# Down-projections over all inner tiles in one span, with four PSUM banks open for each product

## The chip, the core and the metric

The kernel runs on one core of a Trainium2 chip. TensorE (PE in the profile) multiplies into PSUM, VectorE (DVE), ScalarE (ACT) and GpSimd (POOL) work on tiles in SBUF and PSUM, SyncE (SP) issues the loads and stores. The metric is the device time of one execution in microseconds; below, the median of three runs and one profiled execution.

## The reference

Two transformer blocks in a row on 1024 tokens of 1024 features, all in float32. The first has a sliding-window attention beside a gated convolution, the second three kinds of attention and a cross attention. Each ends in a gated feed-forward part with 2816 inner features, whose last product is what the change is about:

```python
# first block
hn = rms_norm(h, ffn_pre_g)
ff = (jax.nn.silu(hn @ w_gate) * (hn @ w_up)) @ w_down
h = h + rms_norm(ff, ffn_post_g)
...
# second block
h = _rmsnorm(x, norm_ffn[l])
gate, up = jnp.split(h @ w_gu[l], 2, axis=-1)
x = x + (jax.nn.silu(gate) * up) @ w_down[l]
...
return _rmsnorm(x, final_norm)
```

## The kernel before

Activations lie with features on the 128 partitions and 512 tokens (one half) in a tile. For precision every operand of a product is split: `hi` is a cast on ACT (L162, L422), `lo` a subtraction of two SBUF operands on DVE or POOL (L163 for weights, L423 for activations), and `mm3` (L530 on) makes each product of three matmuls: hi by hi, hi by lo, lo by hi (L533, L534, L535).

`lower` (L1376) is the down-projection; it is called at L1603 ("down1", into new tiles `ffacc`) and at L2091 ("down2", added to the residual `res`). Its input, 22 inner tiles of two halves, comes from DRAM (`z`), its weights from a stream in DRAM, in pieces of 4 inner tiles by 128 columns (`W.quarter`, called weight quarters below). It takes Winograd's form of Strassen's algorithm: rows are the two halves of the tokens, the inner dimension has two halves, columns come in pairs, four pairs `q`; seven products replace eight. Their operands are sums of x tiles (tiles `s1` and `ff` on DVE, L1398) and differences of weight quarters (`wt`, `wraw`, DVE, L174).

The 22 inner tiles are taken in three chunks, `CHUNKS`, of 8, 8 and 6: in each, `seven` runs all seven products, here named by their evictions: w1 (`ev1`), w5, w6, w7, w4, and the two last with the plain quarters, w3 and w2. Every product makes for each `q` one PSUM bank of 4 (or 3) inner tiles, 12 (or 9) matmuls in a row, and evicts it: a copy to `u` or to the result on ACT (L1455, L1450), or an addition on DVE (L1398); the sums `c += u` of `ev6` and `ev7` are on POOL (`plus`, L1401), in the last chunk on DVE. A chunk loads each operand once: 92 loads for all three. Which engine splits is set by two lists: weights of `q` in `BYDVE` on DVE, x tiles of number `k` in `XDVE` on DVE, the rest on POOL.

What sets the order: the code emits a stage's operands one stage ahead of its matmuls (`AHEAD` = 1), evictions are emitted with a raised priority (`EVP`), and a scheduler orders each engine's queue by that; every engine then takes its queue in order. Loads all go through SP's one queue. Pools bound how far operands run ahead: 8 raw weight quarters (`wq`), 8 each of split ones (`whi`, `wlo`), 7 PSUM banks (`mm`).

When the last chunk's w4 is done, the half of the tokens that is complete goes on: `then(1)` (`to_second` with the post-norm and the residual, reloaded from DRAM by `reload`, or `finish` with the last norm) is emitted before w3's matmuls; `then(0)` follows the end. In the second call the last product's last chunk runs in two pieces of 256 columns (`TAIL`), so that the last norm starts on the first piece.

Of the kernel before, what the change touches and what calls it, by code (L numbers as in the profile page):

```python
# [17 lines left out]
P = 128  # L18
# [8 lines left out]
CHUNKS = ((0, 4), (8, 4), (16, 3))  # L27
AHEAD = 1
PIPE = "fcm"
BYDVE = (3,)  # L30
XDVE = (1, 3)
# [9 lines left out]
BUFS = {'v': 39, 'u': 8, 'p': 4, 'g': 4, 'mm': 7, 's': 3, 't': 3, 'o': 2, 'tmp': 3, 'evt': 3, 'stg': 2, 'rbc': 3, 'turn': 2, 'pt': 2, 'small': 20, 'csmall': 8, 'wraw': 3, 'whi': 8, 'wlo': 8, 'x': 58, 'y': 16, 'ge': 9, 'wt': 6, 'wq': 8, 'r': 16, 'sum': 4, 'rsum': 3, 'f': 6, 'l': 3}  # L41
NPRE = (4, 2)
TAIL = 2
# [37 lines left out]
# float32 values of 10000 ** (-arange(0, 32, 2) / 32)  # L81
# [16 lines left out]
class Weights:  # L98
    """Weights arrive as one stream of 128x128 blocks in the order of their use."""

    def __init__(self, tc, pool, stream):
        self.tc = tc
        self.nc = tc.nc
        self.last = None
        self.marks = {}
        self.pool = pool
        self.stream = stream
        self.order = []
        self.cur = None
        self.made = 0  # L110
# [4 lines left out]
    def in_turn(self, start):  # L115
        """Loads in the order of the stream."""
# [30 lines left out]
    def quarter(self, mat, k, c0, n=4):  # L147
        """n feature tiles of one column of blocks, as they come."""
        while len(self.order) % 4:
            self.order.append(None)  # L150
        s = len(self.order) // 4
        raw = self.pool.tile([P, 512], F32, tag="wq", name=f"wraw{s}", bufs=BUFS["wq"])[:, :n * P]
        self.load(raw, s, n * P)
        self.order += [(mat, k + i, c0) for i in range(n)] + [None] * (4 - n)
        return raw

    def parted(self, raw, eng=None):
        self.made += 1
        w = raw.shape[-1]
        hi = self.pool.tile([P, 512], F32R, tag="whi", name=f"xhi{self.made}", bufs=BUFS["whi"])[:, :w]  # L160
        lo = self.pool.tile([P, 512], F32R, tag="wlo", name=f"xlo{self.made}", bufs=BUFS["wlo"])[:, :w]
# [16 lines left out]
class Act:  # L178
    """Feature tiles of an operand, split: tile k, token half h -> 512 columns hi, 512 lo."""
# [17 lines left out]
class Rows:  # L197
    """Feature tiles in float32: tile i, token half h -> 512 columns."""
# [14 lines left out]
def weave(main, jobs, per=1.0, start=0):  # L213
    """Emits main's steps with jobs between them: per jobs for each step after the first ones."""
# [39 lines left out]
def merged(main, side, n):  # L254
    """main's steps, with a step of side after every n of them."""
# [7 lines left out]
def piped(makers, depth=1):  # L263
    """Jobs from makers of generators: each starts one and takes the ones before a step on."""
# [19 lines left out]
def encoder_decoder_kernel(ctx: ExitStack, tc: tile.TileContext, a: dict, order_out: list):  # L284
# [25 lines left out]
    def act(name, place="vv"):  # L310
        """place: the kind of slot, a letter for each half, or a function of tile and half."""
# [26 lines left out]
    # constants and columns: slices of two tiles (one of matrix operands); the columns go round  # L338
# [71 lines left out]
    flip = [0]  # L410

    def copy(dst, src):
        """PSUM to SBUF, on the two engines in turn."""
# [6 lines left out]
    def split(hi, lo, src, eng=None):  # L420
        """src = hi + lo exactly, both in 12 significant bits."""
# [3 lines left out]
    class Squares:  # L425
        """Sum of squares of [128, w] tiles; side: in two accumulators until the last one."""
# [32 lines left out]
    class Running:  # L459
        """Sums of squares taken as the rows leave PSUM, for each half."""  # L460
# [23 lines left out]
    def rstd(acc, dim, r=None, psum=sps, late=None):  # L484
        """(column sums of acc / dim + eps) ** -0.5: r [128 tokens, tiles], and on every
# [1747 lines left out]
```

## Time and profile before

| | |
|---|---|
| median of 3 runs | 2506.37 us (2502.11 to 2509.57) |
| profiled execution, span | 2505.9 us |
| PE busy | 2372.9 us, 95% |
| DVE busy | 1894.8 us, 76% |
| POOL busy | 1641.7 us, 66% |
| ACT busy | 1015.9 us, 41% |
| first down-projection | from 908 to 1155 us |
| second down-projection | from 2241 to 2492 us |

The shares are means over many stages. A matmul of 512 columns takes 0.23 us when PE runs dense at the full clock; a longer spacing is a wait or a lower granted clock. For one stage, the table of stretches is to be read: busy time of each engine in it, the clock, and what the loads moved.

### The profile page before, as it was taken

To read this page: it belongs to the slowest core of one execution; us is meant where nothing else is said; L and a number is where in the kernel's file an instruction comes from. 1 tells how busy PE (TensorE), PEld (TensorE's weight loads), DVE (VectorE), ACT (ScalarE), POOL (GpSimd) and SP (SyncE) were. 2 spreads that over 40 slices of the span, in tenths; PEclk is the share of its full clock that TensorE was granted. 3 is DMA by queue.
4 is the path that set the end of the run, shared out by engine and by line. 5 is a ranking of instruction groups with operands and counts; after the bars stand their busy time and mean duration, and the time that the engine had idled before them with its cause. 6 is when DMAs were issued, how large, how long until landed. Compare 5 with 4: busy or idle time off the path is not lost.

```text
span 2505.9 us, 34363 instructions
## 1 busy us (share of the span) xinstructions
PE 2372.9 (95%) x11892; PEld 1908.6 (76%) x11892; DVE 1894.8 (76%) x2784; ACT 1015.9 (41%) x2088; POOL 1641.7 (66%) x1194
## 2 busy tenths in 40 slices
PE   8788999889999999998999999999999999998987
PEld 7666777668888877776878778888878888876766
DVE  7989768999555589999443465676799555579988
ACT  5344754533232243435444353544533222334433
POOL 4657557998766669877522334164489666668885
PEclk9888999999999999999999999999999999999998
DMA  4211126423232233232653448113213222253221
GB/s 144 76 34 34 39 81 213 148 72 118 86 104 80 88 123 105 86 121 95 205 154 113 146 121 280 39 51 95 89 59 105 80 76 88 85 190 103 77 73 67
DMA packets 141421, 259.62 MB, mean 104 GB/s; under 512 B 15712, under 2 KB 28352, under 8 KB 141248
## 3 DMA queue, kind: packets, MB, share of 16 engines
q1 hardware_dynamic: 134512, 235.34, 28.9%
q0 software_dynamic: 6448, 21.91, 2.8%
q8 instruction: 94, 1.54, 0.3%
q14 instruction: 79, 0.65, 0.1%
q10 hardware_dynamic: 288, 0.18, 0.0%
HBM read 188.42 MB, written 68.94 MB: 103 GB/s over the span
## 4 chain that ended last, share of the span: by engine, by line
PE 59%; DVE 14%; issue 3%; POOL 2%; ACT 1%; DMA 1%; SPq 0%; DVEq 0%; POOLq 0%; ACTq 0%
PE p L535 10%; PE p L533 10%; PE p L534 10%; PE mm L533 4%; PE mm L534 4%; PE mm L535 4%; DVE s L1398 2%; PE tp L584 2%; PE low L535 2%; PE low L534 2%; PE low L533 2%; DVE ff L423 2%; DVE wt L174 1%; PE lo L1885 1%; DVE ffacc L1398 1%
## 5 line engine op out<-in xcount | busy, mean ns | idle before, releaser
L163 POOL TENSOR_TENSOR xlo<-wt,xhi 128x512 fp32r<-128x512 f32 (+1 forms) x230 | 358.1, 1575 | 31.7 <-ACT xhi L162 24.0
L163 POOL TENSOR_TENSOR xlo<-wraw,xhi 128x512 fp32r<-128x512 f32 (+1 forms) x204 | 321.3, 1588 | 26.5 <-ACT xhi L162 24.1
L140 POOL TENSOR_TENSOR wlo<-wraw,whi 128x512 fp32r<-128x512 f32 x144 | 205.7, 1437 | 142.1 <-ACT whi L139 120.5
L533 PE MATMUL p<-s,xhi 128*128 128x512 f32 x704 | 278.3, 396 | 1.3 <-DVE u L1292 1.0
L535 PE MATMUL p<-s,xlo 128*128 128x512 f32 x704 | 277.7, 396 | 0.9 <-POOL xlo L163 0.9
L534 PE MATMUL p<-s,xhi 128*128 128x512 f32 x704 | 278.0, 395 | 0.0
L535 PE MATMUL low<-ff,xlo 128*128 128x512 f32 (+1 forms) x628 | 252.9, 403 | 25.2 <-POOL xlo L163 25.2
L534 PE MATMUL low<-ff,xhi 128*128 128x512 f32 (+1 forms) x628 | 251.2, 400 | 6.6 <-DVE ff L423 4.5
L533 PE MATMUL low<-ff,xhi 128*128 128x512 f32 (+1 forms) x628 | 250.5, 400 | 5.5 <-DVE u L1398 3.7
L1301 POOL TENSOR_TENSOR g<-g,rbc 128x512 f32<-128x512 f32 x82 | 116.4, 1421 | 188.2 <-ACT g L1300 188.2
L1300 ACT ACTIVATE g<-g 128x512 f32<-128x512 f32 x82 | 51.9, 633 | 422.2 <-DVE g L1299 413.6
L533 PE MATMUL p<-x,xhi 128*128 128x512 f32 x528 | 210.2, 398 | 5.6 <-ACT early L1300 4.9
L535 PE MATMUL p<-x,xlo 128*128 128x512 f32 x528 | 210.6, 399 | 1.1 <-POOL xlo L163 1.1
L534 PE MATMUL p<-x,xhi 128*128 128x512 f32 x528 | 210.0, 398 | 0.1
L162 ACT CAST xhi<-wt 128x512 fp32r<-128x512 f32 (+1 forms) x248 | 142.6, 606 | 144.0 <-DVE wt L174 103.7
L535 PEld LDWEIGHTS low<-ff,xlo 128*128 128x128 f32 x628 | 122.1, 194 | 59.3 <-POOL xlo L163 32.7
L533 PEld LDWEIGHTS p<-s,xhi 128*128 128x128 f32 x704 | 132.8, 189 | 33.4 <-ACT xhi L162 1.4
L535 PEld LDWEIGHTS p<-s,xlo 128*128 128x128 f32 x704 | 132.6, 188 | 32.6 <-POOL xlo L163 1.8
L534 PEld LDWEIGHTS p<-s,xhi 128*128 128x128 f32 x704 | 132.9, 189 | 31.2
L534 PEld LDWEIGHTS low<-ff,xhi 128*128 128x128 f32 x628 | 122.3, 195 | 35.9 <-DVE ff L423 5.8
L533 PEld LDWEIGHTS low<-ff,xhi 128*128 128x128 f32 x628 | 122.1, 194 | 34.3 <-issue 4.2
L162 ACT CAST xhi<-wraw 128x512 fp32r<-128x512 f32 (+1 forms) x228 | 129.6, 599 | 36.4 <-POOL xlo L163 13.5
(446 smaller groups left out, 6445.9 us busy)
## 6 DMA issues: line engine op xcount, KB each, us to landing
wraw<-wstream SPq DMA_DIRECT2D x408, 256.0 KB, 3.0
ff<-zff SPq DMA_DIRECT2D x88, 256.0 KB, 3.5
zff<-up SPq DMA_DIRECT2D x76, 256.0 KB, 2.0
res<-zres SPq DMA_DIRECT2D x48, 256.0 KB, 5.4
x<-xT SPq DMA_DIRECT2D x32, 256.0 KB, 5.4
zres<-res SPq DMA_DIRECT2D x32, 256.0 KB, 2.0
lqk<-zl POOLq DMA_DIRECT2D x16, 512.0 KB, 6.3
wraw<-wstream SPq DMA_DIRECT2D x32, 192.0 KB, 3.1
```

The costliest lines, as they stand in the source:

```text
L140: self.last_part = nc.gpsimd.tensor_tensor(lo, raw, hi.bitcast(F32), op=ALU.subtract)
L162: self.nc.scalar.copy(hi, raw)
L163: ins = (eng or self.nc.gpsimd).tensor_tensor(lo, raw, hi.bitcast(F32), op=ALU.subtract)
L174: self.nc.vector.tensor_tensor(t, a, b, op=ALU.subtract)
L423: return (eng or nc.gpsimd).tensor_tensor(lo, src, f32(hi), op=ALU.subtract)
L533: nc.tensor.matmul(ps, lhsT=ah, rhs=bh, start=first and i == 0, stop=False)
L534: nc.tensor.matmul(ps, lhsT=ah, rhs=bl, start=False, stop=False)
L535: nc.tensor.matmul(ps, lhsT=al, rhs=bh, start=False, stop=last and i == n - 1)
L584: nc.tensor.transpose(ps[:, tsl(j)], pr[:, c0 + (g + j) * P:][:, :P], ident)
L1300: nc.scalar.activation(t, t, AF.Silu)
L1301: nc.gpsimd.tensor_tensor(t, t, rb_[h], op=ALU.mult)
L1398: nc.vector.tensor_tensor(out, x_, y_, op=op)
```

## The change

The chunks go. `lower` runs the seven products once, each over all 11 tiles of its inner half, in three groups of operands of 4, 4 and 3 tiles. The four column pairs' banks are open together through a product (132 matmuls), and are evicted once, at its end: 48 evictions in a down-projection, not 144. Operands are no longer kept: each product loads what it needs when it needs it, 96 weight quarters and 99 x tiles for each down-projection (before 48 and 44). Only the running differences of the weights (new pool `wk`, 12 quarters) and the sums `s_` are kept and updated in place. `plus` is gone: all `c += u` are on DVE, but for four copies in the first call. `BYDVE` and `XDVE` grow: DVE splits two of four weight quarters and three of four x tiles (`k % 4`). `then(1)` is queued before w3 as before; the residual is reloaded in two parts, in w4 and in w3. In the second call the last product is kept whole (46 tiles of split operands) and runs in two pieces of 256 columns. Comments are cut, which moves line numbers: the split of activations is L428, of weights L168, differences L179, the sums and evictions on DVE L1406.

```diff
-CHUNKS = ((0, 4), (8, 4), (16, 3))
-BYDVE = (3,)
-XDVE = (1, 3)
+BYDVE = (1, 3)
+XDVE = (1, 2, 3)
...
-            ins = split(hi, lo, t, nc.vector if k in XDVE else nc.gpsimd)
+            ins = split(hi, lo, t, nc.vector if k % 4 in XDVE else nc.gpsimd)
...
-        def plus(out, x_, y_, op=ALU.add):
-            nc.gpsimd.tensor_tensor(out, x_, y_, op=op)
...
-                def products():
                     for q in Q4:
-                        hi, lo = wparts[q]
-                        ps = mmps("low")
-                        mm3(ps, [((hi[:, tsl(k)], lo[:, tsl(k)]), parts[k]) for k in K])
-                        with tc.high_priority(offset=EVP):
-                            evac(q, ps)
...
+        def w1(g, q):
+            t[g, q] = block(0, 0, g, q, "wk")
+            return t[g, q]
+
+        def w5(g, q):
+            return W.difference(block(0, 1, g, q), t[g, q], t[g, q])
+
+        def w6(g, q):
+            return W.difference(block(1, 1, g, q), t[g, q], t[g, q])
+
+        def w7(g, q):
+            b22 = block(1, 1, g, q)
+            return W.difference(b22, block(0, 1, g, q), b22)
...
+        def x5(k):
+            s_[k] = load(k, 1)
+            return vec(s_[k], s_[k], load(n + k, 1))
...
+        def ev7(q, ps):
+            vec(u[q], u[q], ps)
+            vec(c(q, 3), c(q, 3), u[q])
+            if fresh:
+                nc.gpsimd.tensor_copy(c(q, 2), u[q])
+            else:
+                vec(c(q, 2), c(q, 2), u[q])
...
+        def operands(w_, x_, g, keep):
+            xs = [parted(x_(k), k) for k in groups[g]]
+            ws = []
+            for q in Q4:
+                into = (xt("wk", F32R), xt("wk", F32R)) if keep else None
+                ws.append(W.parted(w_(g, q), nc.vector if q in BYDVE else None, into))
+            return ws, xs
...
+        def whole(parts, g, ps, ev, done):
+            for q in Q4:
+                if g == 0:
+                    ps[q] = mmps("low")
+                group(ps[q], q, g, parts)
+                if g == G[-1]:
+                    with tc.high_priority(offset=EVP):
+                        ev(q, ps[q])
...
+        for w_, x_, ev, done in products:
+            ps, kept = {}, []
+            if done == 1:
+                soon(lambda: then(1))
+            for g in G:
+                keep = tail and done == 0
+                parts = operands(w_, x_, g, keep)
...
+                if keep:
+                    kept.append(parts)
                 else:
+                    soon(lambda parts=parts, g=g, ps=ps, ev=ev, done=done:
+                         whole(parts, g, ps, ev, done))
```

PE before, inside a product of the first down-projection: the last two inner tiles of one bank, then the next bank from its first tile on (`low_8513` and `low_8527` are banks, `ff` the x parts, `xhi` and `xlo` the weight parts).

```order
L533 MATMUL low_8513<-ff_8357,xhi_8373 128x512
L534 MATMUL low_8513<-ff_8358,xhi_8373 128x512
L535 MATMUL low_8513<-ff_8357,xlo_8374 128x512
L533 MATMUL low_8513<-ff_8361,xhi_8373 128x512
L534 MATMUL low_8513<-ff_8362,xhi_8373 128x512
L535 MATMUL low_8513<-ff_8361,xlo_8374 128x512
L533 MATMUL low_8527<-ff_8349,xhi_8377 128x512
L534 MATMUL low_8527<-ff_8350,xhi_8377 128x512
L535 MATMUL low_8527<-ff_8349,xlo_8378 128x512
```

PE after, at the switch from w6 to w7 in the first down-projection: the last matmuls of w6's banks `low_8662` to `low_8701`, and the first of w7's `low_8999` to `low_9038`.

```order
L539 MATMUL low_8662<-ff_8732,xhi_8738 128x512
L540 MATMUL low_8662<-ff_8731,xlo_8739 128x512
L539 MATMUL low_8675<-ff_8732,xhi_8745 128x512
L540 MATMUL low_8675<-ff_8731,xlo_8746 128x512
L539 MATMUL low_8688<-ff_8732,xhi_8752 128x512
L540 MATMUL low_8688<-ff_8731,xlo_8753 128x512
L539 MATMUL low_8701<-ff_8732,xhi_8759 128x512
L540 MATMUL low_8701<-ff_8731,xlo_8760 128x512
L538 MATMUL low_8999<-ff_8816,xhi_8852 128x512
L538 MATMUL low_9012<-ff_8816,xhi_8861 128x512
L538 MATMUL low_9025<-ff_8816,xhi_8870 128x512
L538 MATMUL low_9038<-ff_8816,xhi_8879 128x512
```

The four banks now take each inner tile in turns and close within eight matmuls; before, one bank closed every twelve.

DVE after, at the same switch: w6's evictions (`u` less a bank, then `ffacc` plus `u`) and what stands between and behind them; `ff_8811` is w7's first x tile, `xlo` are weight splits, `wraw` weight differences.

```order
L428 TENSOR_TENSOR ff_8732<-ff_8413,ff_8731 128x512
L1406 TENSOR_TENSOR u_7925<-u_7925,low_8662 128x512
L1406 TENSOR_TENSOR u_7926<-u_7926,low_8675 128x512
L1406 TENSOR_TENSOR ffacc_8565<-ffacc_8565,u_7925 128x512
L1406 TENSOR_TENSOR u_7927<-u_7927,low_8688 128x512
L1406 TENSOR_TENSOR ff_8811<-ff_8811,ff_8813 128x512
L168 TENSOR_TENSOR xlo_8978<-wraw_8972,xhi_8977 128x512
L1406 TENSOR_TENSOR u_7928<-u_7928,low_8701 128x512
L1406 TENSOR_TENSOR ffacc_8578<-ffacc_8578,u_7926 128x512
L179 TENSOR_TENSOR wraw_9186<-wraw_7953,wraw_9186 128x512
```

The first x tile of the new product is made behind three evictions and an addition. ACT after, at the switch before, from w5 to w6 (`ffacc` copies are w5's evictions, `ff_8501` is the first x cast of w6):

```order
L1456 COPY ffacc_8563<-low_8343 128x512
L1456 COPY ffacc_8565<-low_8343 128x512
L167 CAST xhi_8644<-wraw_8007 128x512
L1456 COPY ffacc_8576<-low_8356 128x512
L1456 COPY ffacc_8578<-low_8356 128x512
L167 CAST xhi_8651<-wraw_8013 128x512
L1456 COPY ffacc_8589<-low_8369 128x512
L1456 COPY ffacc_8591<-low_8369 128x512
L427 CAST ff_8501<-ff_8167 128x512
```

The x cast stands behind six copies and two weight casts. POOL in the middle of the first down-projection, before and then after:

```order
L163 TENSOR_TENSOR xlo_9118<-wt_8747,xhi_9117 128x512
L1401 TENSOR_TENSOR ffacc_8176<-ffacc_8176,u_8629 128x512
L423 TENSOR_TENSOR ff_9294<-ff_9081,ff_9293 128x512
L1401 TENSOR_TENSOR ffacc_8193<-ffacc_8193,u_8630 128x512
L163 TENSOR_TENSOR xlo_9122<-wt_8749,xhi_9121 128x512
```

```order
L428 TENSOR_TENSOR ff_8933<-ff_8927,ff_8932 128x512
L168 TENSOR_TENSOR xlo_9190<-wraw_9186,xhi_9189 128x512
L168 TENSOR_TENSOR xlo_9204<-wraw_9200,xhi_9203 128x512
L428 TENSOR_TENSOR ff_9057<-ff_9051,ff_9056 128x512
L168 TENSOR_TENSOR xlo_9305<-wraw_9301,xhi_9304 128x512
```

The additions to `ffacc` are gone from it, and fewer splits are left.

## Rows read from the trace of the kernel before

**Rows 1.** The page's head and its busy times by engine.
```profile
span 2505.9 us, 34363 instructions
PE 2372.9 (95%) x11892; PEld 1908.6 (76%) x11892; DVE 1894.8 (76%) x2784; ACT 1015.9 (41%) x2088; POOL 1641.7 (66%) x1194
```

**Rows 2.** Stretches: length, busy PE, PEld, DVE, ACT, POOL, clock, DMA share, GB/s.
```profile
700.00:880.00 180.00, 180.00 (x784) 146.05 (x783) 102.45 (x135) 53.56 (x99) 118.96 (x83) 1.00 0.26 88
908.00:1156.00 248.00, 226.44 (x946) 179.17 (x944) 234.82 (x252) 105.25 (x198) 205.91 (x135) 0.97 0.30 96
1156.00:1240.00 84.00, 77.22 (x467) 65.10 (x468) 60.29 (x65) 39.06 (x64) 61.56 (x47) 1.00 0.60 196
...
2240.00:2492.00 252.00, 229.10 (x1000) 182.37 (x998) 240.27 (x269) 99.78 (x189) 203.35 (x129) 0.96 0.26 85
...
2230.00:2240.00 10.00, 10.00 (x45) 8.07 (x44) 8.80 (x9) 4.53 (x8) 8.07 (x6) 1.00 1.04 379
```

**Rows 3.** Splits of L423 from 908 to 1156: min/median/max ns, first and last start.
```profile
L423 POOL TENSOR_TENSOR ff<-ff,ff x22: 1288/1746/1842, 936.2 to 1118.3; 128x512 fp32r<-128x512 f32 x22
...
L423 DVE TENSOR_TENSOR ff<-ff,ff x18: 675/1776/1801, 936.7 to 1117.4; 128x512 fp32r<-128x512 f32 x18
```

**Rows 4.** The tile `low`, whole span, and what ended its engines' idle time.
```profile
L533 PE MATMUL low<-ff,xhi x628: 274/394/632, 908.2 to 2491.1; 128*128 128x512 f32 x151, 128*128 128x256 f32 x6
...
L1398 DVE TENSOR_TENSOR u<-u,low x48: 672/674/690, 944.8 to 2468.4; 128x512 f32<-128x512 f32 x48
...
L1398 DVE TENSOR_TENSOR ffacc<-ffacc,low x36: 672/675/689, 972.1 to 1155.5; 128x512 f32<-128x512 f32 x36
...
L1450 ACT COPY ffacc<-low x12: 589/614/652, 918.3 to 939.1; 128x512 f32<-128x512 f32 x12
...
  POOL xlo L163: 57.8, 31
```

**Rows 5.** Groups by line, DVE and POOL, 908 to 1156: busy us, mean ns, idle before.
```profile
L1398 DVE TENSOR_TENSOR ff<-ff,ff 128x512 f32<-128x512 f32 x11 | 13.8, 1258 | 0.1
...
L1398 DVE TENSOR_TENSOR ffacc<-ffacc,u 128x512 f32<-128x512 f32 x12 | 8.6, 759 | 0.0
...
L1401 POOL TENSOR_TENSOR ffacc<-ffacc,u 128x512 f32<-128x512 f32 x20 | 33.7, 1691 | 2.4 <-DVE u L1398 2.4
```

**Rows 6.** Chain that ended last: start us, us, what; three rows from the middle.
```profile
994.68 1.70 DVE s L1398
996.90 1.19 DVE xlo L163
998.09 1.70 DVE ff L1398
```

**Rows 7.** Waits of PE, then of SP, 908 to 1156: us, times, longest.
```profile
PE low L535 <- POOL xlo L163: 13.0, 7, 4.7
PE bc L494 <- DVE sum L448: 4.4, 1, 4.4
...
SPq L113 <- POOL xlo L163: 47.6, 5, 16.6
```

**Rows 8.** Stretches inside the first down-projection, columns as in rows 2.
```profile
1137.00:1143.00 6.00, 1.57 (x15) 1.03 (x13) 5.90 (x9) 3.31 (x6) 2.42 (x3) 0.96 0.31 107
1143.00:1149.00 6.00, 6.00 (x25) 4.83 (x24) 3.78 (x6) 3.44 (x7) 5.09 (x5) 0.50 0.00 0
...
1000.00:1100.00 100.00, 93.00 (x385) 74.05 (x384) 92.96 (x105) 40.35 (x77) 85.56 (x55) 0.97 0.31 93
```

**Rows 9.** The page's DMA issues: count, KB each, us from issue to landing.
```profile
wraw<-wstream SPq DMA_DIRECT2D x408, 256.0 KB, 3.0
ff<-zff SPq DMA_DIRECT2D x88, 256.0 KB, 3.5
```

More of the change, by code (lines that the diff above doesn't have):

```diff
@@ L108, in __init__ @@
         self.order = []
+        self.slots = {}
         self.cur = None
@@ L1163, in park, with unpark @@
         return z
-    def unpark(z):
-        res = rows("res")
-        for h in (0, 1):
+    def unpark(z, halves=(0, 1), res=None):
+        res = res or rows("res")
+        for h in halves:
             for i in range(8):
@@ L1374, in gated, with lower @@
         return z, mark
-    def lower(z, mark, down, acc, run_, fresh, then, ahead=None, before_last=None):
+    def lower(z, mark, down, acc, run_, fresh, then, ahead=None, again=None):
         late = [None, None]
+        n = NFF // 2
+        groups = [range(g, min(g + 4, n)) for g in range(0, n, 4)]
+        G, Q4 = range(len(groups)), range(4)
         def xt(name, dt=F32):
@@ L1530, in lower, with c, block @@
-        queued = []
-        for n0, n in CHUNKS:
-            for products in seven(n0, n, fresh and n0 == 0, n0 + 2 * n == NFF):
-                queued.append(products)
-                if len(queued) > AHEAD:
-                    queued.pop(0)()
-        for products in queued:
-            products()
+            return out
+        def c(q, j):
+            return acc(2 * q + j % 2, j // 2)
+        def block(row, col, g, q, tag="wq"):
+            ks = groups[g]
+            return W.quarter(down, n * row + ks[0], (2 * q + col) * P, len(ks), tag)
@@ new lines, in operands, with group @@
+        def operands(w_, x_, g, keep):
[5 more added lines that the diff above has]
+            return ws, xs
+        def group(ps, q, g, parts, cols=slice(0, HALF)):
+            ws, xs = parts
+            hi, lo = ws[q]
+            mm3(ps, [((hi[:, tsl(i)], lo[:, tsl(i)]), (xs[i][0][:, cols], xs[i][1][:, cols]))
+                     for i in range(len(xs))], first=g == 0, last=g == G[-1])
@@ new lines, in whole, with pieces @@
+        def whole(parts, g, ps, ev, done):
[6 more added lines that the diff above has]
+                        ev(q, ps[q])
+                        if done is not None:
+                            run_.add(done // 2, c(q, done), nc.vector if done > 1 else None)
+        def pieces(parts):
+            w, ends = HALF // tail, []
+            for p_ in range(tail):
+                cols = slice(p_ * w, p_ * w + w)
+                ps = {}
+                for g in G:
+                    for q in Q4:
+                        if g == 0:
+                            ps[q] = mmps("low")[:, :w]
+                        group(ps[q], q, g, parts[g], cols)
+                        if g == G[-1]:
+                            with tc.high_priority(offset=EVP):
+                                d = c(q, 0)[:, cols]
+                                vec(d, d, ps[q])
+                                run_.piece(0, d, cols, q == 3)
+                ends.append(then(0, cols))
+            for e in ends:
+                e()
@@ L1538, in lower @@
+        if ahead:
+            ahead()
+        for f in queued:
+            f()
+        if tail:
+            pieces(kept)
+        else:
+            then(0)
         return late[1]
@@ L1592, in encoder_decoder_kernel, with reload @@
     hm = act("hm")
-    def reload():
-        nx["x"] = unpark(zres)
+    def reload(part):
+        nx["x"] = unpark(zres, (1 - part,), nx.get("x"))
     def to_second(h):
```

177 lines of the change are left out of this document (66 added, 111 removed).

## Prediction

> **What bounds the kernel now.** I read the table of stretches first, then the rows of the splitting line, the rows of the tile that the change concerns, and last the chain and the waits. Sums are made against the profiled span, 2505.9 us [rows 1]; the median of the three runs is 2506.4, so what lies around the span is under a microsecond, and I carry differences over as they are.
>
> PE is busy for 95% of the span [rows 1], which says nothing on the two down-projections. In a gate stage PE runs dense: 784 matmuls in 180.0 us [rows 2], 0.2296 us each at clock 1.00. A down-projection needs 924 of them (7 products x 4 column pairs x 11 inner tiles x 3 terms): 212.2 us. The second, with some of its matmuls as pieces of 256 columns for the tail, needs as much. But the first `low` matmul starts at 908.2 and the first down-projection's last eviction at 1155.5 [rows 4]: 247 us, 35 more than dense; the second fills the stretch from 2240 to 2492 [rows 2], 251 us of it from its first to its last matmul, 38.5 more. What can be won is there: 73.5 us, and some of the 6.8 us in which PE idles from 1156 to 1240 [rows 2].
>
> What takes the place of PE? From 908 to 1156 DVE is busy 234.8 of 248 us and POOL 205.9 [rows 2], and both run slower than they can: a DVE subtraction of two SBUF operands takes 675 ns at best and 1776 in the median, a POOL one 1288 and 1746 [rows 3], whereas DVE operations with one PSUM operand never leave 672 to 690 ns [rows 4]. So the pair competes for reading SBUF, and a POOL operation costs the pair 1.776 - 0.675 = 1.10 us beside the DVE's 0.675. Count the two-SBUF operations of one down-projection in the code: POOL 104 wide and 21 of 384 columns, DVE 137 and 23, and 12 sums of squares (9 on DVE, 3 on POOL). With narrow ones at 0.8 of a wide one (my estimate): 104 x 1.10 + 21 x 0.88 + 137 x 0.675 + 23 x 0.54 + 9.4 = 247 us. That is the whole stage: the common reading path of DVE and POOL is the bound. The chain is made of such rows [rows 6], and PE's longest sum of idle time ends on POOL's split [rows 4].
>
> The Trainium skill ("SBUF — State Buffer", section "Who interferes with whom") says that such a pair is held as an exclusive lock for a whole instruction and the other fully blocks. By that a pair would take 1.29 + 0.675 = 1.96 us rather than the 1.776 of [rows 3], today's sum would be 271, over the 247 that the stage takes, and the sum after the change 217 rather than the 205 below; the row shows a softer rule, and I use the row.
>
> **The change part by part.**
> Partial sums stay in PSUM over 11 inner tiles. Of 144 evictions in a down-projection 96 go, and with them POOL's 20 additions of the first two chunks [rows 5]; 8 (first) or 12 (second) such additions are left, on DVE.
> Splits move. X splits go from 42 POOL and 35 DVE to 21 and 56, weight splits from 63 and 21 to 42 and 42. The 44 sums of x tiles and 48 differences of weights stay on DVE. The common path then has POOL 49 x 1.10 + 14 x 0.88 = 66 (133 before), DVE 168 x 0.675 + 30 x 0.54 = 130 (105 before) and the same 9.4: 205 us, under PE's 212. So the bound passes to PE, by a small margin, and not evenly: by the same prices the three products w5, w6, w7 that need a sum and a difference each take 34 us of it against PE's 30.3 (132 x 0.2296), the others 19 to 26. That excess, 10 us in a down-projection, is bounded by nothing (the splits run up to some 70 matmuls ahead) and by 10; I take it as hidden in the switches, which come next and stop PE in the same products.
>
> Product switches are new. Before, a bank got 12 matmuls in a row and its eviction lay beside the next bank's. Now the four banks take the tiles in turns, and all four close within the product's last 7 matmuls, 1.4 us. The order listing shows what stands in line then. At the switch to w6 in the first down-projection ACT has six eviction copies and two casts ahead of the first x cast: 6 x 0.614 [rows 4] + 2 x 0.6 + 0.6 for the cast = 5.5 us from 1.4 us before the switch, so PE waits about 4.1. At the switch to w7 DVE has three evictions at 0.675, an addition at 0.76 [rows 5] and the x sum at 1.26 [rows 5] in line, then ACT's cast 0.6: 4.6 us, so 3.2, and POOL's split of the same tile (1.3 to 1.75 [rows 3]), covered by four matmuls (0.9) alone, adds 0.4 to 0.8. I price both at 4. At the switch to w4 POOL's copies of u stand ahead of an x split: 2. At the others the operands stand further ahead of the evictions: 0, with 2 each as the upper end. That is 10 us of waits in each down-projection, with bounds 0 (buffers of the earlier groups cover it) and 24 (4 at all six switches).
>
> Waits that stay: the `bc` product waits 4.4 us for sums of squares [rows 7], and as much will be left in each: 4.
>
> Each wait also costs clock. After the wait from 1137 to 1143 the granted clock is 0.50 until 1149, the lower of the two levels (1.2 GHz), and from 1000 to 1100 the 385 matmuls take 93.0 us where 88.4 would do, with 7.0 us idle [rows 8]: 0.66 us more for each idle one; over the whole stretch 9 us in 21.6 idle, 0.43 [rows 2]. I take 0.6. So 14 us of waits make 22.
>
> Loads. Each operand is loaded for each use: 96 weight loads and 99 x loads instead of 48 and 44, 195 in some 235 us, one per 1.2 us. SyncE issues them in order, a load lands after 3.0 to 3.5 us [rows 9], and already today SyncE waits for buffers (47.6 us for one releaser alone [rows 7]). The total of 52 MB is 220 GB/s; the densest product, w7, wants 46 loads, 11.4 MB, in 30.3 us: 377 GB/s, which 2230 to 2240 already shows, 379 [rows 2]. I cost the loads at nothing: the weight loads stand far ahead in the queue, and the waits for the x tiles are in the switch price; if that cover fails it is the last rival.
>
> By the Trainium skill ("SBUF — State Buffer", "Summary: rules for kernel authors") about 358 GB/s is to be had between HBM and SBUF. By it w7 would take 31.9 rather than 30.3 us, 1.6 more in each down-projection; the 379 of [rows 2] is over the figure, and I leave it out.
>
> The tail: the second down-projection's last product, kept whole, runs in two pieces of 256 columns. 264 matmuls of half the columns, at half of 0.2296, are the 30.3 us of the 132 whole ones: dense stays at 212.2 (my estimate; a start cost for each would add a microsecond or two). `then(1)`, the post-norm of the half that is ready, starts before product w3 and has the last two products beside it, some 60 us, about what it had; in the first down-projection it puts some 20 us of the common path beside them, which have 4 to 12 us each to spare: covered in part, and the rest is in the 4 us kept above. What it finishes earlier no longer crowds 1156 to 1240, worth 0 to 6.8; I take 3. The residual's reload in two halves moves 16 loads earlier, at nothing.
>
> Sum: first 212.2 + 22.4 = 234.6 instead of 247.2, a gain of 12.6; second the same instead of 251, 16.4; 3 behind the first. 2506 - 32 = **2474 us**.
>
> **The rivals.**
> *PE dense but for `bc`.* The switches are covered: 16 us less in each down-projection, 2442; with no wait left at all 2425. For: before, PE's operands were 65 to 85 matmuls ahead of their need in the order, and after still 37 to 75 inside a product. Against: 3 to 13 at all switches but the first. 0.18.
> *DVE becomes the serial bound.* DVE does 130 us of two-operand work, 14 to 22 of evictions and 10 of squares, and if each of POOL's 63 operations blocks it for the full 1.10, 66 more: 220 to 228. If it then also stands at the switches for PE's last banks, 2 us at each of six, and has the 20 us of the first half's post-norm in the first: 252 and 240, hence 2497; with half of the blocking it is no different from my forecast. For: DVE is at 95% now [rows 2]. Against: it blocks for only some 64 us on 125 POOL operations now (234.8 less 171 of its own at best). 0.19.
> *Slower: every switch costs as much as the two I worked out.* 6 x 4 + 4 = 28 us of waits, with the clock 45: 257 us each, 2522. It decides from 3.0 us at each switch on, where waits of 22 us with their clock give the 35 us of today. For: the evictions are put ahead of other work, and DVE and ACT take their queues in order. Against: at the first switch the operands are 100 matmuls ahead, and at the last three 9 to 13, 2 to 3 us that the wait is shorter by. 0.10.
> *Slower: loads one by one.* There are 21 groups of operands; a group that begins to load only when its buffers come free shows up to 3.3 landing + 1.3 sum + 0.6 cast + 1.5 split = 6.7 us. If a third of it is seen by PE, 2.2 us, each down-projection has 51 us of waits, 81 with the clock: 2595. It decides from 0.85 us a group. For: one queue in order, and eight slots for raw weights, which one group of w7 fills. Against: w5 to w7 alone have two loads per operand. 0.08.
> That the change doesn't do what it says is excluded by the order: four banks, 132 matmuls each product, 48 evictions.
>
> **How the numbers follow.** My forecast, 2450 to 2490, has 0.45; switches covered (2425 to 2450) 0.18; DVE serial (2490 to 2510) 0.19; the slower ones 0.10 and 0.08. The range leaves out most of the slower ones and the very end below: 2430 to 2512; the likeliest case's own is 2450 to 2490. A measurement here tells 0.3% from no change, that is 2499 to 2514. Faster: 0.45 + 0.18 + half of 0.19 = 0.72; same: the other half and a few hundredths of the slower switches, 0.13; slower 0.15.
>
> **What would show it.** In the table of stretches the two down-projections take 235 us each, with PE busy some 221 and clock 0.97, DVE about 215 and POOL under 110. The median of POOL's splits stays near 1.75, but there are half as many. PE's waits name x splits or casts at the switches to w6 and w7, some 4 us each, and matmuls at half clock behind them; elsewhere under 1 us. SyncE's waits for buffers go up, and loads still land in 3 to 4 us. I am wrong on the switches if PE's waits fall evenly over a product (then it is the common path or the loads: loads if DVE and POOL idle with it, the path if DVE stays over 95%), and wrong on the path if POOL's splits wait while DVE has time.

## The result: 2534 us, 1.1% slower

The changed kernel takes 2534.1 us (median of four runs, 2532.5 to 2537.9) against 2507.2 before: 1.0114 times as long, with a 95% interval of 1.0102 to 1.0127. Forecast were 2474 us and a range of 2430 to 2512; the time lies above it, and on the other side. The profiled execution has a span of 2536.1 us, 30.2 more than in [rows 1].

The page of the changed kernel, busy times by engine and two groups of DMA issues (mean size, then median us to landing):

```profile
PE 2387.6 (94%) x11988; PEld 1917.4 (76%) x11988; DVE 1774.7 (70%) x2736; ACT 1012.6 (40%) x2072; POOL 1425.8 (56%) x1066
...
wraw<-wstream SPq DMA_DIRECT2D x472, 256.0 KB, 3.1
ff<-zff SPq DMA_DIRECT2D x198, 256.0 KB, 4.6
```

DVE is 120 us less busy and POOL 216 us less, as meant. The time is longer all the same, so over the whole kernel neither engine's work is what bounds it now. The stretches of the two down-projections, columns as in rows 2: first whole, then by product. A product's stretch begins with its first matmul and so holds the wait for the next product's first; dense it would be 30.3 us.

```profile
905.00:1179.60 274.60, 239.21 (x981) 183.91 (x980) 199.30 (x246) 109.64 (x204) 114.41 (x83) 0.94 0.54 183
2260.00:2525.60 265.60, 232.75 (x1096) 186.69 (x1094) 187.64 (x253) 97.92 (x185) 101.02 (x66) 0.96 0.51 171
```
```profile
905.00:935.60 30.60, 30.60 (x134) 24.86 (x133) 24.24 (x30) 10.76 (x21) 11.27 (x8) 1.00 0.77 273
935.60:977.60 42.00, 32.75 (x134) 23.91 (x133) 31.25 (x41) 19.26 (x38) 12.34 (x9) 0.99 0.54 182
977.60:1013.70 36.10, 33.64 (x132) 26.81 (x132) 26.81 (x34) 14.06 (x26) 12.62 (x9) 0.92 0.55 179
1013.70:1051.60 37.90, 34.80 (x132) 26.58 (x133) 30.89 (x41) 12.54 (x23) 11.33 (x9) 0.91 0.59 200
1051.60:1088.10 36.50, 31.37 (x133) 24.55 (x133) 23.84 (x27) 14.21 (x27) 18.80 (x15) 1.00 0.57 194
1088.10:1144.00 55.90, 40.45 (x174) 28.71 (x172) 47.71 (x63) 26.67 (x49) 28.78 (x20) 0.88 0.56 193
1144.00:1180.00 36.00, 36.00 (x149) 28.80 (x150) 14.95 (x16) 12.52 (x25) 19.28 (x14) 0.95 0.23 66
```

These are w1, w5, w6, w7, w4, w3, w2 of the first down-projection. w1, whose operands need no sum and no difference, runs dense. w5 to w4 each lose 6 to 12 us, w3 loses 26. In the second one w1 to w3 take 31.6, 39.5, 33.3, 41.0, 35.9 and 46.7 us, and w2's two pieces 37.2. From first to last `low` matmul the two take 273.6 and 265.1 us, 26 and 14 more than before. Around them little has moved: the first starts 3 us earlier, between the two 4 us are gained, and behind the second another 4. That is the whole difference.

In both, PE waits for operands on every path, for ACT's casts of x tiles most. The waits of PE, first and then second down-projection:

```profile
PE low L538 <- ACT ff L427: 22.5, 14, 3.3
PE low L539 <- POOL ff L428: 7.8, 5, 4.2
PE low L539 <- DVE ff L428: 5.0, 4, 2.4
```
```profile
PE low L538 <- ACT ff L427: 12.2, 9, 4.0
PE low L539 <- POOL ff L428: 9.2, 7, 4.6
PE low L539 <- DVE ff L428: 5.7, 4, 2.9
PE low L538 <- ACT wk L167: 5.0, 3, 4.5
```

DVE meanwhile is busy 199 of 275 us and POOL 114. In [rows 2] it was 235 and 206 of 248. The splits of x tiles in the first down-projection (min/median/max ns, first and last start) are faster than in [rows 3], where the medians were 1776 on DVE and 1746 on POOL:

```profile
L428 DVE TENSOR_TENSOR ff<-ff,ff x53: 677/692/1793, 911.5 to 1155.7; 128x512 fp32r<-128x512 f32 x53
...
L428 POOL TENSOR_TENSOR ff<-ff,ff x19: 1265/1432/1753, 921.1 to 1151.8; 128x512 fp32r<-128x512 f32 x19
```

The kernel before was short of DVE and POOL; the changed one has time left on both and is short of operands at the right moment.

### The profile page after: what moved, and what is told of

Read it like the earlier page. It is cut to its first block, busy times and chain, and to the rows that moved or that the text cites. A ratio compares the mean times of both kernels' runs of the same rounds, so it can differ in the third digit from the quotient of the medians.

```text
span 2536.1 us, 34653 instructions
## 1 busy us (share of the span) xinstructions
PE 2387.6 (94%) x11988; PEld 1917.4 (76%) x11988; DVE 1774.7 (70%) x2736; ACT 1012.6 (40%) x2072; POOL 1425.8 (56%) x1066
## 4 chain that ended last, share of the span: by engine, by line
PE 45%; DVE 6%; issue 2%; DMA 2%; POOL 2%; ACT 1%; SPq 0%; DVEq 0%; ACTq 0%; POOLq 0%
PE p L540 5%; PE p L538 5%; PE p L539 5%; PE mm L538 4%; PE mm L540 4%; PE mm L539 4%; PE low L539 2%; PE low L538 2%; PE low L540 2%; PE tp L589 2%; PE lo L1916 1%; PE fo L603 1%; DMA wraw<-wstream 1%; DVE ff L1406 1%; DVE xlo L168 1%
## 5 line engine op out<-in xcount | busy, mean ns | idle before, releaser
L168 POOL TENSOR_TENSOR xlo<-wraw,xhi 128x512 fp32r<-128x512 f32 (+1 forms) x210 | 325.9, 1564 | 157.7 <-ACT xhi L167 103.6
L168 POOL TENSOR_TENSOR xlo<-wt,xhi 128x512 fp32r<-128x512 f32 x176 | 268.1, 1541 | 39.7 <-issue 10.7
L539 PE MATMUL low<-ff,xhi 128*128 128x512 f32 x572 | 235.5, 413 | 27.7 <-POOL ff L428 17.0
L540 PE MATMUL low<-ff,xlo 128*128 128x512 f32 x572 | 232.1, 407 | 0.0
L538 PE MATMUL low<-ff,xhi 128*128 128x512 f32 x572 | 174.3, 409 | 34.8 <-ACT ff L427 34.7
L427 ACT CAST ff<-ff 128x512 fp32r<-128x512 f32 x154 | 93.2, 618 | 242.8 <-DVE ff L1406 198.7
L167 ACT CAST xhi<-wraw 128x512 fp32r<-128x512 f32 (+1 forms) x288 | 160.7, 597 | 36.1 <-PE p L540 16.8
L539 PEld LDWEIGHTS low<-ff,xhi 128*128 128x128 f32 x572 | 112.3, 196 | 65.1 <-POOL ff L428 23.7
L538 PEld LDWEIGHTS low<-ff,xhi 128*128 128x128 f32 x572 | 107.8, 193 | 69.8 <-ACT ff L427 46.8
L540 PEld LDWEIGHTS low<-ff,xlo 128*128 128x128 f32 x572 | 112.1, 196 | 25.2
```

Source lines behind the costliest of these rows:

```text
L167: self.nc.scalar.copy(hi, raw)
L168: ins = (eng or self.nc.gpsimd).tensor_tensor(lo, raw, hi.bitcast(F32), op=ALU.subtract)
L427: nc.scalar.copy(hi, src)
L538: nc.tensor.matmul(ps, lhsT=ah, rhs=bh, start=first and i == 0, stop=False)
L539: nc.tensor.matmul(ps, lhsT=ah, rhs=bl, start=False, stop=False)
L540: nc.tensor.matmul(ps, lhsT=al, rhs=bh, start=False, stop=last and i == n - 1)
```

## The experiments

The theories: the **switch** (the four evictions of a product stand ahead of the next product's operands), the **loads** (three times as many x loads, one queue in order), the **path** (DVE and POOL still too slow), and, after the first runs, **work beside** (operands are now made one product at a time, so whatever else runs beside a product delays it). Times of products are from first matmul to first matmul of the next. A gap at a switch is the time between the starts of two matmuls less the usual 0.23 us; the wait that a row of the profile shows for it is some 0.2 us shorter.

**Stores out of the loads' way (e1).** In w3, SyncE stands for 20.9 us at a store of the residual in the first down-projection, and 22.5 us at an output store in the second, with operand loads behind it. SyncE's waits around w3, first and then second:

```profile
SPq L1167 <- POOL res L1134: 27.4, 6, 20.9
...
SPq L2104 <- POOL yo L2098: 23.9, 3, 22.5
```

That looked like the cause.

```diff
-    zres2 = park(nx["x"], "zres2")
+    zres2 = park(nx["x"], "zres2", loads["last"])
...
+                    if h:
+                        held.append(lambda out=out, y=y: nc.sync.dma_start(out, y))
+                        continue
```

> The changed kernel with only the place of 32 stores in SyncE's queue moved: the stores that park the residual (first down-projection) and the 8 output stores of the first half (second one, written in place and stored from the residual tiles) come after the last operand load instead of between the loads of w3 and w2. Queue theory (operand loads stand behind stores whose data come from POOL: 20.9 and 22.5 us of waits of SyncE, and product w3 takes 55.9 and 46.8 us where others take 36): w3 falls to 36 to 40 in both, 20 to 26 us less in all, 2508 to 2514. Switch theory (evictions ahead of operands make the loss): the stores do not matter, 2530 to 2536. Path theory (DVE and POOL): w3 has the post-norm beside it and stays long, 2528 or more.

2536.5 us, no change. The waits at the stores are gone, and w3 takes 58.4 and 45.3 us:

```profile
1087.30:1145.70 58.40, 42.62 (x173) 30.66 (x171) 46.59 (x63) 26.65 (x49) 28.35 (x20) 0.82 0.44 140
2446.90:2492.20 45.30, 35.63 (x154) 26.85 (x152) 29.39 (x41) 17.47 (x34) 14.54 (x12) 0.92 0.32 103
```

A long wait in a queue, with the right work behind it, was no evidence: with it gone, w3 stays as long. The row to read in the first down-projection was DVE's busy time, 46.6 of 58.4 us, with 63 operations where w5 to w7 have 34 to 41: the post-norm of the ready half. In the second DVE is busy only 29.4 of 45.3 us, so there that row doesn't tell.

**The split lists undone (e2), and alone in the kernel before (e3).**

```diff
-BYDVE = (1, 3)
-XDVE = (1, 2, 3)
+BYDVE = (3,)
+XDVE = (1, 3)
```

> The changed kernel with the two lists of the splits as before (a quarter of the weight splits and about half of the x splits on DVE). Path theory: the common path takes 42 more POOL operations at 1.10 for 42 DVE ones at 0.675, 18 us more in each down-projection: 2560 to 2570. Queue and switch theory: DVE is not full in the changed kernel (31 of 42 us busy in w5), the loss comes from late loads or evictions, and the lists move less than 8 us: 2526 to 2542.

2543.7 us, 9.5 more than the changed kernel. The lists help, by about a third of what the path theory said (26 to 36). They do not help everywhere: with the old lists w5 of the first down-projection is 3.1 us shorter than in the changed kernel, and w7 1.5 and 4.6; w4 and w3 are each about 2 longer.

The same lines the other way round in the kernel before:

> The kernel before with only the two lists of the change (half of the weight splits, three of four x tiles on DVE). Path theory: 42 splits from POOL to DVE save 42 x 0.42 = 18 us of the common path in each down-projection: 2470 to 2480. If DVE in its own order is what is full (busy 234.8 of 248 us), moving work to it gives nothing or costs: 2500 to 2520.

2493.6 us, 0.9944 times the kernel before (0.9927 to 0.9962): faster than both kernels. The down-projections take 236.2 and 239.2 us instead of 247.2 and 250.9. So the new lists are the good part of the change, and all else in it costs about 41 us. The stretch of the first one:

```profile
908.00:1143.50 235.50, 220.66 (x938) 174.18 (x936) 234.40 (x284) 103.55 (x197) 147.12 (x94) 0.98 0.33 103
```

DVE is full here (234.4 of 235.5 us), POOL no longer.

**Fewer loads (e4).**

```diff
-            return vec(s_[k], s_[k], load(n + k, 1))
+            return vec(s_[k], s_[k], s_[k])
...
-            return vec(x11, x11, load(k, 1), ALU.subtract)
+            return vec(x11, x11, s_[k], ALU.subtract)
...
-            return W.difference(b22, block(0, 1, g, q), b22)
+            return W.difference(b22, t[g, q], b22)
```

> The changed kernel with one load for each operand of w5 (x) and w7 (x and weights); the second source of each sum or difference is a tile that is there already, so those operands have wrong values. 34 of 195 loads fall away in each down-projection, all other instructions stay. Queue theory: w5 (41.9 and 39.5 us) and w7 (37.9 and 41.0) come down to 33 to 36, 15 to 22 us less in all: 2512 to 2519. Switch theory: the gaps at the switches to w6 and w7 (3.5, 2.7+2.9; 1.4+2.1, 4.1+1.9) stay, and the total falls by under 6: 2528 to 2534. Path theory: no change, since every DVE and POOL operation is there.

2527.8 us, 6.3 less, between the two. w5 in the first goes from 41.9 to 37.8 us; in the second it and w7 in the first stay; w7 in the second goes from 41.0 to 38.6. The gaps at the switches stay.

**The post-norm behind the products (e5).**

```diff
-            if done == 1:
-                soon(lambda: then(1))
...
+        with tc.issue_after(prior[0].ins):
+            then(1)
```

> The changed kernel with the post-norm of the ready half moved: in the first down-projection its first PE product comes after the last matmul of w2, in the second after the last matmul of w3 (before the tail's pieces). Beside theory (w3 takes 55.9 and 46.8 us because the post-norm's 40-odd operations of DVE and POOL stand among operand work that is now still to be done): w3 falls to 33 to 37 us in both; the first down-projection ends after 250 to 256 us instead of 274, but the post-norm is then bare, some 20 us behind it, so the total is 2525 to 2540. Switch theory: w3 stays over 45, since its evictions and its first operands are where they were; the total rises by 20 or more.

2527.4 us, 6.7 less. w3 falls from 55.9 and 46.7 to 36.0 and 38.9 us, and PE's waits in it to almost nothing; its stretches, and the one behind the first down-projection, where the post-norm now runs bare at a clock of 0.78:

```profile
1087.40:1123.40 36.00, 31.87 (x134) 24.26 (x132) 28.99 (x38) 17.15 (x33) 13.28 (x10) 0.99 0.70 233
2436.40:2475.30 38.90, 32.66 (x153) 25.22 (x151) 26.67 (x37) 17.39 (x34) 11.63 (x10) 0.98 0.19 60
1157.00:1180.00 23.00, 17.23 (x88) 12.94 (x85) 21.08 (x24) 12.04 (x20) 18.09 (x12) 0.78 0.24 91
```

So 28 us of the loss in the two w3 come from the post-norm beside them. Put elsewhere it costs most of that again: between the two down-projections 16 us are lost.

**One bank after the other (e6).** PE's order is forced within a group.

```diff
+            with tc.issue_after(prior[0].ins) if prior[0] else nullcontext():
+                prior[0] = mm3(ps, [((hi[:, tsl(i)], lo[:, tsl(i)]), (xs[i][0][:, cols], xs[i][1][:, cols]))
+                         for i in range(len(xs))], first=g == 0, last=g == G[-1])
```

> The changed kernel with PE's order forced: within a group of 4 (or 3) inner tiles one bank after the other, 12 (or 9) matmuls in a row as in the kernel before. The four banks then close 2 us apart over 6 us instead of within 1.4 us, and an x tile has to be there at the start of a group. Switch theory: the gaps at the switches to w6 and w7 (3.5 and 5.6; 3.5 and 6.0 us) fall by half or more, 10 to 20 us less in all with the clock: 2515 to 2525. If instead the operands of a product come late because they are made one product at a time, whatever the order in which they are used: no change or slower, since four x tiles are wanted at once, 2532 to 2560.

2539.9 us, 5.8 more. The gaps at the switches are gone, and waits of the same size stand within the first group, where a bank wants four x tiles at once. w6 gets 2.7 us shorter, w7 2.9 longer in the first down-projection. It tells only that this order of PE does not mend it.

**Loads for each use in the kernel before (e8)**, with both new lists.

```diff
+            x11 = [load(n0 + k, 0) for k in K]
...
+            b22, b12 = weights(1, 1), weights(0, 1)
+            x11 = [load(n0 + k, 0) for k in K]
+            x21 = [load(n0 + k, 1) for k in K]
...
+            b21 = weights(1, 0)
+            x12 = [load(n0 + n + k, 0) for k in K]
```

> The kernel before with both lists of the change, and with each operand loaded again for each use: 96 weight loads and 99 x loads in a down-projection, as in the changed kernel, but with its three chunks, its banks and its evictions. Load theory: the loads are what the changed kernel pays for, 2515 or more against 2493.6. If they are hidden (the run with 34 loads fewer gained 6 us): 2488 to 2503.

2505.8 us, 12 more than with the lists alone. 195 loads instead of 92 in a down-projection are not free, and not the main loss. In the traces most of the difference doesn't even lie where the loads are: from first to last `low` matmul the two down-projections take 238.9 and 239.0 us, against 236.2 and 239.2 with the lists alone. Behind the second 5 us are lost and between the two 2; why is not shown.

**Two groups ahead (e9).**

```diff
-            if len(queued) > AHEAD:
+            if len(queued) > 2:
...
+                if not keep and g == 1:
+                    into = [W.pool.tile([P, 512], F32R, tag=tg, name=nm(tg), bufs=BUFS[tg]) for tg in ("lhi", "llo")]
```

> The changed kernel with two groups of operands made ahead of PE instead of one, and four more buffers each for the high and low parts of the weights. Look-ahead theory (the products w5 to w4 take 36 to 42 us because a product's operands start to be made only when the product before is nearly done): w5 to w4 fall to 31 to 35 us in both down-projections, 20 to 35 us less: 2500 to 2515. Work theory (w5 to w7 need more of DVE's and POOL's time than PE's 30 us each, whenever they begin): a small gain, 2525 to 2533, since only the beginning moves.

2537.9 us, nothing gained; neither theory had that. w5 gets 5 us shorter in each, and w1 5 and 8 us longer: work that is begun earlier seems to delay what stands there.

**No weight differences (e10).**

```diff
-            return W.difference(block(0, 1, g, q), t[g, q], t[g, q])
+            return block(0, 1, g, q)
```

and the same in w6, w7 and w4.

> The changed kernel without the 48 differences of weights in each down-projection: w5, w6, w7 and w4 take one weight quarter as it is, 12 of 195 loads fall away; the operands have wrong values. Work theory: 48 DVE operations, 12 in each of four products, 8 us alone and up to 20 contended in each: w5 to w4 fall to 31 to 34 us, 30 to 45 us less in all: 2490 to 2505. Look-ahead theory: weights stand far ahead in the queues and the x tiles come late all the same, w5 to w4 stay over 35: 2520 to 2532.

2508.9 us, 25 less, with 12 loads fewer in w7 too. In the first down-projection, w5, w6, w7, w4:

```profile
936.80:970.90 34.10, 30.81 (x134) 24.64 (x133) 15.11 (x17) 14.23 (x28) 11.17 (x9) 0.99 0.53 175
970.90:1007.60 36.70, 33.64 (x132) 26.73 (x132) 25.55 (x31) 13.96 (x26) 13.15 (x9) 0.92 0.61 197
1007.60:1040.70 33.10, 32.75 (x132) 25.75 (x133) 22.08 (x28) 12.56 (x23) 11.68 (x9) 0.95 0.54 169
1040.70:1077.40 36.70, 32.93 (x134) 25.71 (x133) 24.10 (x28) 14.32 (x27) 19.05 (x15) 0.95 0.56 192
```

The two heavy products, w5 and w7, lose 8 and 5 us (8 and 8 in the second); the waits inside them are gone. w6 and w4 stay as they were (w6 of the second gets 5 us longer), and so do the gaps at their switches: two causes, one inside the heavy products and one at the switches.

**No evictions of w6 and w7 (e13).**

```diff
         def ev6(q, ps):
-            vec(u[q], u[q], ps, ALU.subtract)
-            vec(c(q, 1), c(q, 1), u[q])
+            return
 
         def ev7(q, ps):
-            vec(u[q], u[q], ps)
-            vec(c(q, 3), c(q, 3), u[q])
```

> The changed kernel without the evictions of w6 and w7: their banks are not read, u is not updated and not added to the result, only the copy of u in w7 stays (the results lack these two products). The operations, the loads and the order of the operands stay. Eviction theory: the gaps at the switches from w6 to w7 (2.7 and 2.9 us; 4.1 and 1.9) and from w7 to w4 (1.5 and 2.6; 3.0) shrink to under 1 us in all at each, w7 and w4 get 4 to 6 us shorter each with the clock, while the gap from w5 to w6 (3.5; 1.4 and 2.1), whose evictions stay, stays as the control: 2512 to 2522. Late-operand theory: the gaps stay within 1.5 us of what they were and the total falls by under 8 us, 2526 to 2533: the first operands of a product are late by themselves, by loads, sums and casts made in order.

2519.5 us, 14.6 less. Without w6's evictions the gap before w7 is 0 and 1.1 us (2.7 and 2.9 before), without w7's the one before w4 is 0 (4.1), and likewise in the second (6.0 to 2.3, 3.0 to 0). The control stays: the switch from w5 to w6 waits 4.0 and 1.7 (3.5), and 1.4 and 2.7 in the second. w7 and w4 in the first, then in the second:

```profile
1006.00:1041.50 35.50, 32.72 (x133) 24.16 (x133) 29.67 (x37) 13.60 (x26) 12.68 (x10) 1.00 0.82 262
1041.50:1073.40 31.90, 30.79 (x133) 24.61 (x132) 17.31 (x18) 11.46 (x23) 13.79 (x9) 1.00 0.57 182
2352.70:2389.00 36.30, 32.67 (x133) 24.14 (x132) 30.46 (x38) 13.62 (x26) 12.87 (x10) 1.00 0.79 260
2389.00:2419.50 30.50, 30.50 (x134) 24.79 (x132) 18.67 (x16) 11.26 (x22) 15.81 (x10) 1.00 0.43 132
```

w4 runs nearly dense. The eviction theory holds for the switches: 2 to 5 us for each product. The variant also has 16 DVE operations fewer in a down-projection, so not every microsecond is the order's. And its profiled execution took 2513.2 us where its median is 2519.5, that of the changed kernel 2537.9 where its median is 2534.1; so read the gaps rather than the last microsecond of a product.

**A better version: the lists in the kernel before.** Four more of them (e7, e11, e12, e14), since the first was faster than both kernels.

> The kernel before with only the weight list of the change (half of the weight splits on DVE, x splits as before). With both lists it took 2493.6 and DVE was busy 241 of 245 us. Path theory: about half of that gain, 21 of 42 splits, 2499 to 2502. If DVE is already too full with both lists, the half step is better: 2485 to 2493.

2513.3 us: the weight list alone is slower than before, 1.0026 (1.0015 to 1.0038).

> The kernel before with only the x list of the change (three of four x tiles split on DVE, weight splits as before). Both lists gave 2493.6, the weight list alone 2513.3, so that list costs 6 us by itself. If the two add: 2507 - 20 = 2487 (2484 to 2491). If they only work together: 2500 to 2507.

2515.8 us: the x list alone is slower too, 1.0037 (1.0027 to 1.0047).

```diff
-XDVE = (1, 3)
+XDVE = (0, 1, 2, 3)
...
-            if k not in XDVE:
-                late[1] = ins
+            late[1] = ins
```

> The kernel before with all x splits on DVE, weight splits as before. If POOL's x splits are what PE waits for and the common path is the bound, one more step of 42 operations: 2475 to 2490. If DVE's own order is full by then (241 of 245 us busy with both lists): 2495 to 2515.

2500.8 us, 0.9969 (0.9958 to 0.9981).

> The kernel before with the weight list of the change and all x splits on DVE. Each of the two alone gave 2513 and 2501, the weight list with three of four x tiles 2493.6. If POOL's share of the common path still counts: 2484 to 2491. If DVE is full: 2495 to 2510.

2491.3 us, 0.9944 (0.9929 to 0.9959), the fastest time here, and not to be told apart from the 2493.6 of the change's own two lists. Each list alone costs 6 to 10 us and the two together gain 14: their effects do not add. Why is open; each list gives the scheduler another order of every queue, and no run here separates that from the work moved.

## Why the prediction was wrong, step by step

The forecast had 14 us of waits in each down-projection; PE idles 35 and 33. That term of the sum failed, in steps that I put at nothing and in one that I priced too low.

**What bounds the kernel now** was not confirmed. Taking 42 splits from POOL to DVE gains 14 us in the kernel before, less than the sum's 36 for two down-projections, and DVE is then at 234.4 of 235.5 us: its own queue fits as the bound no worse than the common path. Each half of that step alone costs 6 to 10 us, where the path would have gained from both (e7, e11). The price of 1.10 us for a POOL operation is an average of that stage's mixture; it let me carry over 205 us as if it were a free schedule.

**The step that failed first: then(1) "has the last two products beside it, some 60 us, about what it had".** I counted PE's time as the cover. It was not what it had: before, the 72 matmuls of the last chunk's w3 and w2 ran from 1129.8 to 1155 us, 25 us. And by then only the last chunk's operands of those products were left to be made, 3 of 11 tiles. Now they all are still to be made, on the engines that the post-norm needs. I charged nothing for it beyond the 4 us of `bc`; w3 lost 26 and 16 us, and 28 of these 42 go when the post-norm goes (e5). The net price of its place is smaller, since bare it costs most of that again: 6.7 us. I had priced the post-norm's 20 us of common path and set them against slack of 4 to 12 us a product, and then rounded the rest away.

**The second: the 10 us excess of w5, w6, w7 "as hidden in the switches".** Waits inside a product and at its beginning add. I set three products at 34 us of path against PE's 30; w5 and w7 took 38 to 42. With the weight differences left out they take 32 to 34 (e10), and that is 28 us over the two down-projections. But w6, which I had set at 34 as well, took 36 and 33 and did not fall without its differences. So the sum for a product doesn't tell by itself which one comes late; w5 and w7 differ from w6 in having two loads for each x tile, and 34 loads fewer took 4 us from one w5 and 2 from one w7 (e4). The sums were made for 212 us of a stage, where 205 fit. The kernel before mixes heavy and light products every 36 to 48 matmuls; in one span 396 heavy ones stand in a row, and the look-ahead of one group did not smooth that. Nor did two (e9).

**The switches** were the right mechanism, near the right size where I walked the queue, and too low in their sum. The order's reading can be seen word for word in the trace. From 1009.9 us, the switch from w6 to w7:

```profile
1009.90 1.28 DVE L1406 TENSOR_TENSOR u<-u,low 128x512 f32<-128x512 f32 x2 [4.09 <-PE low L540]
...
1010.86 0.39 PE L540 MATMUL low<-ff,xlo 128*128 128x512 f32 x1
...
1011.10 0.69 DVE L1406 TENSOR_TENSOR ffacc<-ffacc,u 128x512 f32<-128x512 f32 x1
...
1011.70 0.68 DVE L1406 TENSOR_TENSOR u<-u,low 128x512 f32<-128x512 f32 x1
1012.30 0.68 DVE L1406 TENSOR_TENSOR ff<-ff,ff 128x512 f32<-128x512 f32 x1
...
1013.07 0.62 ACT L427 CAST ff<-ff 128x512 fp32r<-128x512 f32 x1 [5.91 <-DVE ff L1406]
...
1013.74 1.50 PE L538 MATMUL low<-ff,xhi 128*128 128x512 f32 x4 [2.50 <-ACT ff L427]
1013.77 1.28 POOL L428 TENSOR_TENSOR ff<-ff,ff 128x512 fp32r<-128x512 f32 x1 [5.52 <-ACT ff L427]
```

Three evictions, the addition, the x sum, the cast, and PE has stood for 2.5 us (forecast 3.2); POOL's split behind it adds a little. The line of six copies before w6 cost 3.5 us (forecast 4.1). But the second tile of w7 waits another 2.9, the switches to w4 and to w2 cost 4.1 and 3.1 where I took 2 and 0, and the second down-projection's tail 4.7: 16 and 17 us instead of 10. This alone, with the clock, is about 10 us a stage.

**Loads "at nothing"** was wrong by the 6 to 12 us of e4 and e8. The densest product is the second w1, 2260 to 2291.7, with 337 GB/s; x loads land after 4.6 us, not 3.5 [rows 9]. But the loads were not the cause of w3's loss, though SyncE's row there had the longest single wait of either down-projection. The prediction's own sign would have misled here: waits spread over a product, with time left on DVE and POOL, were to mean the loads.

**The clock** was right in kind. In the first down-projection PE idles for 274.6 - 239.2 = 35.4 us, and its 981 matmuls take 14 us more than at 0.2296 each: 0.4 for each idle microsecond (0.6 taken). It is a mean over unlike stretches: w5 idles 9 us at a clock of 0.99.

**The aftermath**: 3 us forecast, 4 measured.

**The rivals.** "Every switch costs as much" had the sign and 2522 us, and a part of the mechanism: 16 and 17 us of its 24 are there. The greater losses, the post-norm and the heavy products, are not in it; that it came nearest is partly luck. "PE dense" is refuted by the same 16 and 17 us. "Loads one by one" was to give 2595; 34 loads fewer gain 6 us. "DVE becomes the serial bound" had the post-norm's 20 us in it, and would have given 2497; DVE is busy only 73% of the stage, so it is not full, only late. The mean over a stage decided neither.

What stays open: what part of the waits inside w5 is ACT's and DVE's handing to and fro of one tile (sum, cast, split, each in its queue's order), what is DVE's time and what the loads'. It got shorter with work taken away (e10), with loads taken away (e4), with splits moved to POOL (e2) and with an earlier beginning (e9). Nor do the parts add up: e10, e13, e5 and e4 together would give 53 us where the new structure costs 41, and no run takes two of them at once.

## What to carry to other kernels

A budget that fits over a whole stage says little where the work comes in lumps: make the sum for each product with all that stands beside it, and ask of each moved piece not only what covers it but whose operands are still to be made on the same engines. Keeping a sum open in PSUM saves evictions, but it bunches the rest at the switch; read the in-order queue there and walk the chain from the last matmul to the next first one, since that came within a microsecond at the two switches where I walked it. When a change has several parts, run the cheap one alone: two lists of numbers gave 14 us in the old structure, and the new structure lost 41.

## What the runs showed of the hardware

Loads landed later when there were more of them. In the first down-projection, with 183 GB/s instead of 96 in the mean, x loads took 4.6 us instead of 3.0 and weight loads 4.3 instead of 3.5 (KB each, median us to landing; before, then after):

```profile
ff<-zff SPq DMA_DIRECT2D x32, 256.0 KB, 3.0
wraw<-wstream SPq DMA_DIRECT2D x28, 256.0 KB, 3.5
```
```profile
ff<-zff SPq DMA_DIRECT2D x92, 256.0 KB, 4.6
wraw<-wstream SPq DMA_DIRECT2D x55, 256.0 KB, 4.3
```

What they wait for is not shown. And the granted clock fell after some gaps. In the same list of events as above, some 2 us behind the 2.5 us without a matmul:

```profile
1015.69 0.63 PE L540 MATMUL low<-ff,xlo 128*128 128x512 f32 x1
1016.12 0.63 PE L539 MATMUL low<-ff,xhi 128*128 128x512 f32 x1
...
1017.83 0.42 PE L539 MATMUL low<-ff,xhi 128*128 128x512 f32 x1
```

The matmuls follow each other at 0.43 us and take 0.63, where 0.23 and 0.39 are usual. The clock granted there is 0.50, the lower of the two levels (1.2 GHz); five matmuls at that pace cost 1 us more than usual. It didn't fall after every gap: behind one of 2.4 us in w4 it stayed at 1.00. Both stretches, columns as in rows 2:

```profile
1015.69:1017.83 2.14, 2.14 (x7) 1.65 (x6) 2.14 (x4) 0.00 (x0) 0.00 (x0) 0.50 0.90 321
1059.60:1064.60 5.00, 3.70 (x15) 2.74 (x15) 4.90 (x6) 4.76 (x10) 3.31 (x3) 1.00 0.78 263
```
